# Fifteen gate and up weight units split at another address offset, in a hybrid decoder layer on one Trainium2 core

## The chip, the cores and the metric

The kernel runs on one core of a Trainium2 chip. The metric is the device time of one execution in microseconds, taken as the median of the runs. One execution was also recorded by the hardware profiler; its time stands beside its span (from the first to the last instruction).

## The reference, cut to what matters

One layer on 512 tokens of width 2048, in float32: a mixer (an RG-LRU and an RWKV-7 half), a feed-forward network of width 6144, a gated embedding, and norms. The change touches the first half of the feed-forward network:

```python
u = rmsnorm(h, ln_ffn[i])
gate = causal_dwconv(u @ w_gate[i], conv_f_w[i], conv_f_b[i])
h = h + (jax.nn.gelu(gate) * (u @ w_up[i])) @ w_down[i]
```

`w_gate` and `w_up` are 2048 by 6144 each.

## The kernel before, in words

**Precision.** Each product is made of three matmuls in a fast float32 format. An operand is split in a high part (ScalarE copies it to that format, line 138) and a low part (VectorE subtracts the high part from it, line 139). High times high, high times low and low times high are added up in PSUM.

**Stages.** Up to about 908 us the mixer runs, with 512-column matmuls of which the streamed operand is an activation tile `x` and the loaded weights are `whi` and `wlo` (`dense`, lines 173 to 177; in the gates of the RG-LRU, lines 1031 to 1035, the streamed tiles are `lxh` and `lxl`). From about 908 to 1870 us come gate and up. Then come the down projection (`product`, lines 1418 to 1420) and the gated embedding (`gate`, lines 1564 to 1566), to the end at 2575 us.

**Gate and up.** The products with `w_gate` and `w_up` are arranged so that seven products with sums and differences of operand blocks stand for eight plain ones. `gate_order` (line 1122) lists the work in 336 *units* (n, name): n is one of 48 blocks of 128 features, the name one of q5, p1, p4, p6, p7, p2, p3. In `part` (line 1288) a unit is 24 matmuls: for each of eight slices of 128 rows, the weights `whi` are loaded and stream past `xh`, loaded again and stream past `xl`, then `wlo` and `xh`. The streamed tiles `X` (named s in the profile) have 256 columns, and every matmul loads 128 by 128 weights first. The units run in this order on TensorE without a break.

**The feed of the weights.** `wqueue`, `wfill` and `wnext` (lines 105 to 151) hold a list of all weight units of the kernel in the order of their use. For a unit, a raw weight tile of 512 KB is loaded by a transfer of the SP queue, or made by `gate_unit` (line 1129): an addition on VectorE, or a transfer of GpSimd's queue that adds to what is in the tile. Then line 138 writes `whi` and line 139 `wlo`. In this stage three units are kept ahead (LOOK), in three buffers each for `whi` and `wlo` (HL). Every fourth unit (k % 4 == 3, counted from 0) has two tiles of its own, x12 and x15, in place of a buffer.

**The addresses.** A buffer of `whi` or `wlo` has 1088 columns of 4 bytes in each partition, and a unit needs 1024. `wview` (line 142) puts the unit at column `a` of the buffer, with `a` from a table `at` by the unit's place in the list. `ffn_items` (line 1191) fills that table, and line 1204 sets it for the gate and up units. In the compiled program all `whi` and `wlo` buffers start at 128 modulo 256 bytes, x12 and x15 too, and the streamed `X` tiles at 64. So with a = 0 the streamed data lies 64 bytes below the weights, modulo 256 (the *difference* minus 64); with a = 48 (192 bytes) the weights are at 64 as well, difference zero; with a = 56 (224 bytes) the weights are at 96, 32 above the streamed data. x12 and x15 always have minus 64.

In the mixer both `x` and the weights are at 128, difference zero, and `lxh` and `lxl` are at 160, 32 above the weights. In the down projection and the gated embedding the split weights are streamed and the activations are loaded. There a = 48 gives difference zero. In the last part a = 32 puts the streamed weights at 0, with the loaded tiles at 64, so minus 64; and two weight units with tiles of their own (s8, s11) are at 64, difference zero.

**What sets the order around the change.** The order of units is that of `gate_order`. The queue of weights follows it, and each split waits for the buffer of the unit three before it. Line 1204 changes nothing in order, number or size of instructions.

Of the kernel before, what the change touches and what calls it, by code (L numbers as in the profile page):

```python
# [90 lines left out]
class Builder:  # L91
# [1099 lines left out]
    def ffn_items(self):  # L1191
        A = self.A
        u = (128, 8, 128)
        r = []
        direct = {"p1": (0, 0), "p2": (0, 1), "p4": (1, 1)}
        self.gw = {}
        for k, (n, o) in enumerate(self.gate_order()):
            own = (("x12", "x15") if k % 4 == 3 else ())
            if o == "p2" or n == 0 and o in direct or n == 1 and o == "p1":
                i, j = direct[o]  # L1200
                r.append((A["wgu"][n // 2 * 2 + i, n % 2, j], u) + own)
            else:
                r.append((lambda n=n, o=o: self.gate_unit(n, o), u) + own)
        r = [(i, 48 if k in (12, 16, 20) or k % 56 == 4 else 0) for k, i in enumerate(r)]
        u = (128, 2, 512)
        self.d0, self.d1, self.dq, self.pn = {}, {}, {}, 0
        for lo, hi in GROUPS:
            for b in range(2):
                for i in ORDER:
                    for ch in range(lo, hi):  # L1210
                        if i == 5:
                            r.append(((A["wd"][ch, b, 1, 0], u), 48))
                        else:
                            r.append(((lambda ch=ch, c=ch - lo, b=b, i=i: self.down_unit(ch, c, b, i), u), 48))
        r += [((A["wd"][NCH - 1, cb % 2, kh, cb // 2], u), 48) for cb in (0, 2, 1, 3) for kh in range(2)]
        for cb in range(4):
            r += [((A["wpp"][cb], u), 0)]
            if cb < 3:
                r += [((A["wpg"][cb, i], u), 48) for i in KORDER[cb > 0]]
        r += [((A["wpg3"][0, i], (128, 4, 256)), 32) for i in range(2)]  # L1220
        r += [((A["wpg3"][1, 0, :, 2 * i:2 * i + 2], (128, 2, 256), ("s8", "s11")[i]), 0) for i in range(2)]
        r += [((A["wpg3"][0, i], (128, 4, 256)), 32) for i in range(2, 4)]
        r += [((A["wpg3"][1, i], (128, 4, 256)), 32) for i in range(1, 4)]
        return r
# [535 lines left out]
```

## Time and profile before

| | before |
|---|---|
| median of 3 runs | 2575.83 us |
| lowest and highest | 2571.14, 2579.5 us |
| the profiled execution | 2576.38 us |
| its span | 2574.6 us |
| its mean granted TensorE clock | 0.990 |
| ScalarE | 49% busy |
| GpSimd | 9% busy |
| HBM traffic over the span | 152 GB/s |

In a group of the profile, the tile names have lost their numbers: `mm<-s,whi` is a matmul that writes a PSUM tile mm, streams s and has whi loaded. A name x in the place of whi or wlo is x12 or x15, and wk is a second kind of PSUM tile. "128*128" is the size of the loaded weights, and behind it stand the streamed partitions and columns. A row of busy time by stretches has the length, then the busy time and the number of instructions of each engine, the granted clock, the share of the DMA engines and their rate. An instruction that begins before a stretch and ends in it is counted. A row of a timeline has the start, the duration and the instruction.

### The profile page before, as it was taken

To read this page: it belongs to the slowest core of one execution; us is meant where nothing else is said; L and a number is where in the kernel's file an instruction comes from. 1 tells how busy PE (TensorE), PEld (TensorE's weight loads), DVE (VectorE), ACT (ScalarE), POOL (GpSimd) and SP (SyncE) were. 2 spreads that over 40 slices of the span, in tenths; PEclk is the share of its full clock that TensorE was granted. 3 is DMA by queue.
4 is the path that set the end of the run, shared out by engine and by line. 5 is a ranking of instruction groups with operands and counts; after the bars stand their busy time and mean duration, and the time that the engine had idled before them with its cause. 6 is when DMAs were issued, how large, how long until landed. Compare 5 with 4: busy or idle time off the path is not lost.

```text
span 2574.6 us, 51613 instructions
## 1 busy us (share of the span) xinstructions
PE 2517.4 (98%) x21922; PEld 2220.6 (86%) x21922; DVE 1902.3 (74%) x2603; ACT 1248.8 (49%) x1735; POOL 228.0 (9%) x251
## 2 busy tenths in 40 slices
PE   9989999999999989999999999999999999999997
PEld 8767777777777889999999999999988877888887
DVE  5765775776585988888888888888876877896447
ACT  6563654557432644444444444444465453535345
POOL 0010100101031000000000000000000000000001
PEclk9999999999999999999999999999999999999998
DMA  7221222222342567767777677676778686843233
GB/s 256 91 74 59 87 79 68 79 81 73 92 145 83 163 202 196 190 170 192 197 183 190 167 196 194 182 191 181 206 223 240 184 239 177 248 121 122 92 94 111
DMA packets 131448, 393.76 MB, mean 153 GB/s; under 512 B 14481, under 2 KB 26769, under 8 KB 131217
## 3 DMA queue, kind: packets, MB, share of 16 engines
q1 hardware_dynamic: 96624, 299.22, 34.5%
q0 software_dynamic: 19872, 72.36, 16.8%
q10 hardware_dynamic: 14720, 18.88, 2.2%
q8 instruction: 171, 2.80, 0.4%
q14 instruction: 61, 0.49, 0.1%
HBM read 353.97 MB, written 36.44 MB: 152 GB/s over the span
## 4 chain that ended last, share of the span: by engine, by line
PE 59%; DVE 6%; DMA 3%; ACT 2%; issue 2%; POOL 0%; ACTq 0%; POOLq 0%; DVEq 0%; SPq 0%
PE mm L1293 8%; PE mm L1294 8%; PE mm L1292 8%; PE mm L1419 5%; PE mm L1420 5%; PE mm L1418 5%; PE wk L1293 3%; PE wk L1292 3%; PE wk L1294 3%; PE mm L1564 2%; PE mm L1565 2%; PE mm L1566 2%; DVE wlo L139 2%; DMA wraw<-wd 1%; PE mm L173 1%
## 5 line engine op out<-in xcount | busy, mean ns | idle before, releaser
L138 ACT ACTIVATE whi<-x 128x1024 fp32r<-128x1024 f32 x329 | 348.4, 1060 | 472.8 <-PE mm L1293 223.2
L139 DVE TENSOR_TENSOR wlo<-x,whi 128x1024 fp32r<-128x1024 f32 x329 | 401.8, 1222 | 134.2 <-ACT whi L138 130.7
L138 ACT ACTIVATE whi<-wraw 128x1024 fp32r<-128x1024 f32 (+1 forms) x229 | 233.2, 1018 | 388.8 <-PE mm L175 181.1
L1292 PE MATMUL mm<-s,whi 128*128 128x256 f32 x1432 | 403.4, 282 | 3.6 <-ACT whi L138 2.5
L139 DVE TENSOR_TENSOR wlo<-wraw,whi 128x1024 fp32r<-128x1024 f32 (+1 forms) x229 | 279.2, 1219 | 172.4 <-ACT whi L138 170.8
L1294 PE MATMUL mm<-s,wlo 128*128 128x256 f32 x1432 | 403.3, 282 | 0.8 <-DVE wlo L139 0.8
L1293 PE MATMUL mm<-s,whi 128*128 128x256 f32 x1432 | 403.2, 282 | 0.2 <-DVE s L157 0.2
L173 PE MATMUL mm<-x,whi 128*128 128x512 f32 x832 | 332.9, 400 | 2.3 <-DVE tmp L519 1.0
L177 PE MATMUL mm<-x,wlo 128*128 128x512 f32 x832 | 332.7, 400 | 0.0
L175 PE MATMUL mm<-x,whi 128*128 128x512 f32 x832 | 331.0, 398 | 0.0
L1292 PEld LDWEIGHTS mm<-s,whi 128*128 128x128 f32 x1432 | 275.5, 192 | 4.0 <-ACT whi L138 2.7
L1294 PEld LDWEIGHTS mm<-s,wlo 128*128 128x128 f32 x1432 | 269.7, 188 | 1.0 <-DVE wlo L139 1.0
L1419 PE MATMUL mm<-wlo,s 128*128 128x512 f32 x680 | 267.0, 393 | 3.4 <-DVE wlo L139 3.4
L1293 PEld LDWEIGHTS mm<-s,whi 128*128 128x128 f32 x1432 | 269.7, 188 | 0.4 <-DVE s L157 0.4
L1418 PE MATMUL mm<-whi,s 128*128 128x512 f32 x680 | 265.5, 392 | 3.0 <-ACT whi L138 3.0
L1420 PE MATMUL mm<-whi,s 128*128 128x512 f32 x680 | 266.3, 392 | 0.2
L173 PEld LDWEIGHTS mm<-x,whi 128*128 128x128 f32 x832 | 157.5, 189 | 38.1 <-issue 3.0
L177 PEld LDWEIGHTS mm<-x,wlo 128*128 128x128 f32 x832 | 157.2, 189 | 34.2 <-issue 1.9
L175 PEld LDWEIGHTS mm<-x,whi 128*128 128x128 f32 x832 | 157.4, 189 | 33.8 <-issue 1.8
L1158 POOL DMA_DIRECT2D x<-wgu x94 | 82.9, 882 | 936.6 <-DVE wlo L139 632.2
L1292 PE MATMUL wk<-s,whi 128*128 128x256 f32 x584 | 164.2, 281 | 1.3 <-DVE e L1318 1.3
L1293 PE MATMUL wk<-s,whi 128*128 128x256 f32 x584 | 164.1, 281 | 0.0
(579 smaller groups left out, 5417.7 us busy)
## 6 DMA issues: line engine op xcount, KB each, us to landing
x<-wgu SPq DMA_DIRECT2D x144, 512.0 KB, 4.2
x<-wgu POOLq DMA_DIRECT2D x94, 512.0 KB, 5.5
wraw<-wz SPq DMA_DIRECT2D x80, 512.0 KB, 3.5
wraw<-wgu SPq DMA_DIRECT2D x51, 512.0 KB, 4.2
x<-wd SPq DMA_DIRECT2D x49, 512.0 KB, 6.0
x<-wd POOLq DMA_DIRECT2D x44, 512.0 KB, 6.1
wraw<-wpg SPq DMA_DIRECT2D x31, 512.0 KB, 3.5
wraw<-wd SPq DMA_DIRECT2D x30, 512.0 KB, 4.5
```

The lines of the kernel that those rows point to most:

```text
L138: nc.scalar.activation(hi, raw, AF.Copy)
L139: nc.vector.tensor_tensor(lo, raw, hi.bitcast(F32), ALU.subtract)
L173: nc.tensor.matmul(ps, hi[:, k, :], xh, start=first and i == 0, stop=False)
L175: nc.tensor.matmul(ps, hi[:, k, :], xl, start=False, stop=False)
L177: nc.tensor.matmul(ps, lo[:, k, :], xh, start=False, stop=last and i == n - 1)
L1158: nc.gpsimd.dma_start(g["s"], src(0, 0 if u == "p6" else 1), accum_op=ALU.add)
L1292: TE.matmul(ps, wh[:, k, :], xh, start=k == 0, stop=False)
L1293: TE.matmul(ps, wh[:, k, :], xl, start=False, stop=False)
L1294: TE.matmul(ps, wl[:, k, :], xh, start=False, stop=k == 7)
L1418: TE.matmul(ps, x[0][:, k, ts_], w[0][:, k, :], start=first and k == 0, stop=False)
L1419: TE.matmul(ps, x[0][:, k, ts_], w[1][:, k, :], start=False, stop=False)
L1420: TE.matmul(ps, x[1][:, k, ts_], w[0][:, k, :], start=False, stop=last and k == 1)
```

## The change

Line 1204 is replaced:

```diff
-        r = [(i, 48 if k in (12, 16, 20) or k % 56 == 4 else 0) for k, i in enumerate(r)]
+        r = [(i, 56 if k // 4 in (3, 5, 7, 29, 57) and k % 4 < 3 else 0) for k, i in enumerate(r)]
```

Before, nine units have a = 48: 4, 12, 16, 20, 60, 116, 172, 228 and 284. After, none has. Fifteen have a = 56: 12 to 14, 20 to 22, 28 to 30, 116 to 118 and 228 to 230. Each of these five groups is followed by a unit with tiles of its own. All other gate and up units have a = 0.

## The prediction

> **What bounds the kernel now.** I read the page first, then busy time by stretches, then groups of instructions in the stretch that the change touches.
>
> ```profile
> span 2574.6 us, 51613 instructions
> PE 2517.4 (98%) x21922; PEld 2220.6 (86%) x21922; DVE 1902.3 (74%) x2603; ACT 1248.8 (49%) x1735; POOL 228.0 (9%) x251
> ```
>
> ```profile
> core 0: us, PE busy (x) PEld busy (x) DVE busy (x) ACT busy (x) POOL busy (x), PEclk, DMA share, GB/s
> 1000.00:1200.00 200.00, 200.00 (x1700) 200.00 (x1699) 164.61 (x182) 90.08 (x96) 17.57 (x20) 1.00 0.72 190
> 1200.00:1400.00 200.00, 200.00 (x1701) 200.00 (x1700) 163.60 (x181) 90.33 (x96) 18.46 (x21) 1.00 0.70 183
> ```
>
> The changed units run from about 908 to 1870 us. In there TensorE is busy 200 us of 200 at the full granted clock, VectorE 82%, ScalarE 45%, the DMA engines 0.7. The groups of the stretch 960 to 1866 us say who feeds whom:
>
> ```profile
> L1293 PE MATMUL mm<-s,whi 128*128 128x256 f32 x1364 | 383.3, 281 | 0.0
> L1294 PE MATMUL mm<-s,wlo 128*128 128x256 f32 x1364 | 383.3, 281 | 0.0
> ```
>
> ```profile
> L138 ACT ACTIVATE whi<-x 128x1024 fp32r<-128x1024 f32 x207 | 219.4, 1060 | 312.9 <-PE mm L1293 223.2 <-PE wk L1293 89.7
> ```
>
> ```profile
> L139 DVE TENSOR_TENSOR wlo<-x,whi 128x1024 fp32r<-128x1024 f32 x206 | 251.9, 1223 | 81.5 <-ACT whi L138 78.1
> ```
>
> The matmuls wait for nothing (0.0 before them). The split waits for TensorE to free a buffer (312.9 us before ScalarE's part), so the feed has room. The stage is as long as 336 units of 24 matmuls are at their own spacing, and nothing else ends last. A matmul's recorded 281 ns overlaps its neighbours; what counts is start to start. I get that by counting matmuls in stretches whose ends lie between two starts. Two in each count began before the stretch, so the spacing is the length over (count minus 2).
>
> ```profile
> core 0: us, PE busy (x), PEclk, DMA share, GB/s
> 1100.00:1240.00 140.00, 140.00 (x1191) 1.00 0.70 180
> 1248.54:1251.42 2.88, 2.88 (x26) 1.00 1.06 358
> 1251.42:1254.25 2.83, 2.83 (x26) 1.00 0.89 172
> 942.80:945.15 2.35, 2.35 (x22) 1.00 0.00 0
> 951.65:954.24 2.59, 2.59 (x24) 1.00 0.72 174
> 924.52:931.43 6.91, 6.91 (x63) 1.00 0.95 226
> 2513.73:2518.45 4.72, 4.72 (x42) 1.00 0.50 134
> 2521.06:2535.46 14.40, 14.40 (x129) 1.00 0.23 74
> 2538.15:2541.44 3.29, 3.29 (x31) 1.00 0.00 0
> 441.95:443.76 1.81, 1.81 (x10) 1.00 0.15 57
> 444.24:446.34 2.10, 2.10 (x11) 1.00 0.00 0
> ```
>
> All of them ran at clock 1.00. For the 256-column matmul the rows show three spacings that hold steady:
> - 140 us over 1189, 117.7 ns: the gate and up stage at difference minus 64, with none of the nine units in it. Rows 942.80 (117.5) and 951.65 (117.7), and 2513.73 at the end of the kernel (118.0), are the same.
> - 2.88 over 24, 120.0 ns: unit 116, one of the nine at difference zero. The next unit, row 1251.42, is back at 117.9.
> - 6.91 over 61, 113.3 ns, in the same stage, also at minus 64; and 14.40 over 127 and 3.29 over 29, 113.4 ns, in the last part of the kernel at minus 64.
>
> So minus 64 has two gaits, one 4% shorter than the other. Whichever TensorE falls into, it keeps until something disturbs it. From 951 to 1867 us nothing does but the units at zero, and it stays in the long one.
>
> **The change part by part.**
>
> What it removes: nine units at zero go to minus 64 (four of them, units 12, 20, 116 and 228, go to 32). At unchanged gait that is 2.88 − 2.83 = 0.05 us each, 0.45 us for nine. Nothing hides it, because TensorE sets the stage.
>
> What it adds: 15 units at difference 32. No 256-column matmul of before has that difference. The nearest rows are the two last of the list, with 512 columns: at difference zero 1.81 over 8, 226 ns; right behind, with the moving operand 32 above the weights, 2.10 over 9, 233 ns. That is about 7 ns more and no short gait in the stretch. Put on 113.3 this gives 120.3, the spacing of the units at zero, and I take 120: 24 × (120.0 − 117.7) = 0.055 us a unit, 0.8 us for 15. Bounds: below, the short gait holds inside the groups, 24 × 15 × (113.3 − 117.7) = −1.6 us; above, twice the 7 ns, 24 × 15 × (127 − 117.7) = +3.4 us. No instruction, wait or transfer is added or moved; the split of line 138 and 139 runs with another offset in the same buffer. If it cost ScalarE or VectorE more at another address, their idle time above covers it.
>
> So inside the units the whole change is worth under 4 us either way. What decides is the gait in which TensorE leaves a group. Two ways out of difference zero are in the trace. In the gate stage, row 1251.42: long gait (and the same behind the other units at zero from unit 12 on, eight of eight). In the last part each of four runs of 12 matmuls at zero is followed by matmuls at minus 64; the first:
>
> ```profile
> start us, us, engine line op out<-in xcount [idle before <-releaser]
> 2537.26 0.28 PE L1565 MATMUL mm<-s,s 128*128 128x256 f32 x1
> 2537.38 0.28 PE L1566 MATMUL mm<-s,s 128*128 128x256 f32 x1
> 2537.50 0.29 PE L1564 MATMUL mm<-whi,s 128*128 128x256 f32 x1
> 2537.62 0.28 PE L1565 MATMUL mm<-wlo,s 128*128 128x256 f32 x1
> 2537.74 0.28 PE L1566 MATMUL mm<-whi,s 128*128 128x256 f32 x1
> 2537.86 0.28 PE L1564 MATMUL mm<-whi,s 128*128 128x256 f32 x1
> 2537.97 0.28 PE L1565 MATMUL mm<-wlo,s 128*128 128x256 f32 x1
> 2538.09 0.28 PE L1566 MATMUL mm<-whi,s 128*128 128x256 f32 x1
> ```
>
> Steps of 120 ns become 110 to 120 within five matmuls, and row 2538.15 shows the short gait from there on. Same two differences, other result. What differs is which operand moved: here the streamed one went from 64 to 0, in the gate stage the weights go from 64 to 128. A start is therefore decided by where the streamed data and the weights stand at that moment, and a group that ends with the weights at 96 leaves from another place than one that ends at 64. After a wait it is open too:
>
> ```profile
> start us, us, engine line op out<-in xcount [idle before <-releaser]
> 923.77 0.38 PE L1294 MATMUL mm<-s,x 128*128 128x256 f32 x1 [0.63 <-DVE x L139]
> ...
> 951.40 0.36 PE L1292 MATMUL wk<-s,x 128*128 128x256 f32 x1 [0.72 <-DVE e L1318]
> ```
>
> After the first came 113.3, after the second 117.7. Counting by kind: long after 942.8, 951.4, 2513.4 and the units at zero in the gate stage; short after 923.8 and after the runs at zero in the last part. It is near a coin toss for one way out, and I put it a little above half for the short gait, since there are three groups close together and 72 matmuls give each of them time to settle.
>
> The sum for the short gait: units 15 to 335 are 321, less the 12 in the four later groups, 309 units × 24 × (117.7 − 113.3 = 4.4 ns) = 32.6 us less; the groups and the removed nine +0.8 − 0.45 = +0.4. Together −32.2 us.
>
> Can the feed follow? A unit then has 2.72 us instead of 2.83. VectorE's 164.61 us in 200 become 171, ScalarE's 90 become 94, the DMA share 0.72 becomes 0.75. The tightest is the weight that is added up in memory by a transfer of GpSimd's queue:
>
> ```profile
> x<-wgu POOLq DMA_DIRECT2D x90, 512.0 KB, 5.5
> ```
>
> It must land between two splits that are four units apart, 10.9 us then; 5.5 us in the median and the split's 1.06 + 1.22 leave 3 us. I cost that at nothing.
>
> The profiled execution took 2576.38 us, 1.8 us over its span, and lies 0.6 us over the median of the three runs (2575.83, from 2571.14 to 2579.5). From the profiled one the sum is 2544.2; from the median it is 2543.6, and I give 2544. The runs spread over 0.3%, so 7.7 us is what can be told from no change.
>
> On the rule that speaks against the change: the rows just used have spacing depend on the address of the weights, 120.0 against 117.9. The Trainium skill (TensorE: Matmul & The Clock Gate, Part 2, step 1) holds that TensorE has two independent read ports, so that loading the next weights takes nothing from the running matmul. By that rule both spacings would be equal and the change would do nothing; the trace disagrees by 2 ns a matmul.
>
> **The rivals.**
> - *The gait stays long.* Every exit is like row 1251.42: 15 units at 120 instead of nine, 2575.8 + 0.4 = 2576. For it: eight of eight in this stage. Against it: the exits at 2537.5 and the start at 923.8.
> - *Short for a part.* Only the group at unit 116 or 228 turns it, or a later one turns it back: 218 units × 0.106 = 23 us or 105 × 0.106 = 11 us less, 2553 or 2565.
> - *Slower: a third gait.* Behind a group TensorE at minus 64 keeps the 120 ns that it shows at zero: 309 × 24 × 2.3 ns = 17 us more, 2593. It decides from 7.7 us over 321 × 24 matmuls, 1.0 ns, so from 118.7 on. For it: at 444 us the 512-column matmuls kept 233 as long as the difference held. Against it: every settled stretch at minus 64 shows one of the two gaits.
> - *Addresses do nothing.* The 0.05 us at unit 116 would be chance, and the time 2575.8; eight equal units speak against it.
>
> **How the numbers follow.** Short gait from an early group 0.46, short for a part 0.11, long gait 0.34, addresses nothing 0.02, third gait 0.07. Faster by over 0.3%: 0.46 + 0.11 = 0.57. Within: 0.36. Slower: 0.07. The likeliest case alone: 2544 with −1.6 and +3.4 for the groups and ±4 for the runs, 2538 to 2551. The range over the cases reaches up to the long gait with the same additions, 2581, and leaves out the third gait.
>
> **What would show it.** In the changed profile a stretch of 140 us in this stage without a group should hold 140000/113.3 = 1235 matmuls and not 1189; the stage should end near 1834 us instead of 1867; units 116 to 118 should take about 2.88 us each. If the stretches before and after each group hold 1189, the groups don't turn the gait, and I am wrong by 32 us. If short stretches end at a wait on VectorE or a transfer, the feed was the step that failed.

## The result and the profile after

| | before | after |
|---|---|---|
| median of 6 runs each, one chip | 2574.16 us | 2541.42 us |
| lowest and highest | 2571.14, 2579.5 us | 2533.88, 2574.53 us |
| the profiled execution | 2576.38 us | 2544.37 us |

The ratio of the times is 0.9862, with a 95% interval from 0.984 to 0.9884: 1.4% faster. The runs of the changed kernel fall into two groups some 32 us apart, and since a ratio leaves out runs that lie over 1.5% above the fastest, the text also gives the number of runs in each group. Here five lie at 2533.9 to 2544.6 us and one, 2574.53, where the kernel before lies.

The head of the page after:

```profile
span 2542.6 us, 51613 instructions
PE 2486.8 (98%) x21922; PEld 2188.8 (86%) x21922; DVE 1898.9 (75%) x2603; ACT 1250.1 (49%) x1735; POOL 228.2 (9%) x251
```

The same instructions, and TensorE busy for 30.6 us less. Where these went is read from stretches cut at the same places of the program. First the kernel before: its gate and up stage to the start of unit 12 and from there to its end, then, with TensorE alone, the down projection and the last part. In the first two rows stand the length, busy time and number of instructions of TensorE, weight loads, VectorE, ScalarE and GpSimd, then clock, DMA share and GB/s.

```profile
908.53:954.20 45.67, 38.52 (x305) 37.17 (x304) 34.67 (x48) 18.24 (x28) 4.87 (x5) 0.96 0.73 210
954.20:1870.56 916.36, 916.36 (x7779) 916.36 (x7778) 754.60 (x837) 416.82 (x445) 79.98 (x91) 1.00 0.71 187
...
1870.56:2364.53 493.97, 487.37 (x2186) 1.00 0.71 198
2364.53:2574.60 210.07, 193.29 (x1043) 0.97 0.30 98
```

The same stretches of the kernel after:

```profile
908.88:953.04 44.16, 38.51 (x305) 37.33 (x304) 34.60 (x47) 17.95 (x27) 4.85 (x5) 0.96 0.75 220
953.04:1836.15 883.11, 883.11 (x7779) 883.11 (x7777) 750.49 (x837) 417.58 (x445) 79.82 (x91) 1.00 0.74 194
...
1836.15:2332.35 496.20, 488.75 (x2185) 1.00 0.71 198
2332.35:2542.60 210.25, 193.31 (x1043) 0.97 0.31 98
```

From unit 12 on the stage takes 883.11 us in place of 916.36, 33.25 less, with the same 7779 matmuls and TensorE busy throughout. The rest comes to +1.2: −1.5 ahead of unit 12, +2.2 in the down projection, +0.5 elsewhere.

Inside that stretch, TensorE alone (length, busy time and count, clock, DMA share, GB/s; two of each count began before the stretch):

```profile
951.16:953.04 1.88, 1.88 (x18) 1.00 0.89 131
953.04:961.56 8.52, 8.52 (x74) 1.00 0.49 133
961.56:964.30 2.74, 2.74 (x26) 1.00 0.34 88
964.30:975.18 10.88, 10.88 (x98) 1.00 0.90 238
...
1100.00:1240.00 140.00, 140.00 (x1237) 1.00 0.74 196
...
1237.02:1245.54 8.52, 8.52 (x74) 1.00 0.91 259
1245.54:1256.41 10.87, 10.87 (x98) 1.00 0.69 178
```

Unit 11 ends in the long gait (1.88 over 16, 117.5 ns). The first group, units 12 to 14, takes 118.3 ns a matmul (8.52 over 72). Unit 15 needs five or so steps to change over, and units 16 to 19 run at 113.3 (10.88 over 96). The 140 us that held 1189 matmuls before hold 1235. The group at unit 116 costs 118.3 as well, and behind it TensorE is back at 113.3.

How the feed stands, in the groups from 960 to 1834 us:

```profile
L1293 PE MATMUL mm<-s,whi 128*128 128x256 f32 x1365 | 377.2, 276 | 0.0
...
L139 DVE TENSOR_TENSOR wlo<-x,whi 128x1024 fp32r<-128x1024 f32 x206 | 251.4, 1220 | 71.5 <-ACT whi L138 68.3
L138 ACT ACTIVATE whi<-x 128x1024 fp32r<-128x1024 f32 x206 | 218.9, 1063 | 285.1 <-PE mm L1293 199.7 <-PE wk L1293 74.7 <-DMA x<-wgu 8.5
```

The matmuls still wait for nothing, and the split still waits for TensorE, 285 us where it was 313.

### The profile page after: what moved, and what is told of

Read it like the earlier page. It is cut to its first block, busy times and chain, and to the rows that moved or that the text cites. A ratio compares the mean times of both kernels' runs of the same rounds, so it can differ in the third digit from the quotient of the medians.

```text
span 2542.6 us, 51613 instructions
## 1 busy us (share of the span) xinstructions
PE 2486.8 (98%) x21922; PEld 2188.8 (86%) x21922; DVE 1898.9 (75%) x2603; ACT 1250.1 (49%) x1735; POOL 228.2 (9%) x251
## 4 chain that ended last, share of the span: by engine, by line
PE 58%; issue 5%; DVE 4%; DMA 3%; ACT 1%; POOL 0%; ACTq 0%; POOLq 0%; DVEq 0%; SPq 0%
PE mm L1294 8%; PE mm L1293 8%; PE mm L1292 8%; PE mm L1420 5%; PE mm L1419 5%; PE mm L1418 5%; PE wk L1292 3%; PE wk L1294 3%; PE wk L1293 3%; PE mm L1564 2%; PE mm L1565 2%; PE mm L1566 2%; DMA wraw<-wd 2%; DVE wlo L139 1%; ACT whi L138 1%
## 5 line engine op out<-in xcount | busy, mean ns | idle before, releaser
L139 DVE TENSOR_TENSOR wlo<-x,whi 128x1024 fp32r<-128x1024 f32 x329 | 401.1, 1220 | 121.0 <-ACT whi L138 117.5
L1292 PE MATMUL mm<-s,whi 128*128 128x256 f32 x1432 | 396.1, 277 | 1.0 <-ACT s L156 0.9
L1294 PE MATMUL mm<-s,wlo 128*128 128x256 f32 x1432 | 396.0, 277 | 0.8 <-DVE wlo L139 0.8
L1293 PE MATMUL mm<-s,whi 128*128 128x256 f32 x1432 | 396.0, 277 | 0.2 <-DVE s L157 0.2
L1292 PEld LDWEIGHTS mm<-s,whi 128*128 128x128 f32 x1432 | 268.9, 188 | 1.5 <-ACT s L156 1.1
L1294 PEld LDWEIGHTS mm<-s,wlo 128*128 128x128 f32 x1432 | 268.9, 188 | 1.0 <-DVE wlo L139 1.0
L1293 PEld LDWEIGHTS mm<-s,whi 128*128 128x128 f32 x1432 | 269.0, 188 | 0.4 <-DVE s L157 0.4
L1292 PE MATMUL wk<-s,whi 128*128 128x256 f32 x584 | 162.3, 278 | 2.9 <-DVE e L1318 2.9
L1294 PE MATMUL wk<-s,wlo 128*128 128x256 f32 x584 | 162.1, 278 | 0.0
```

The lines of the kernel that those rows point to most:

```text
L139: nc.vector.tensor_tensor(lo, raw, hi.bitcast(F32), ALU.subtract)
L1292: TE.matmul(ps, wh[:, k, :], xh, start=k == 0, stop=False)
L1293: TE.matmul(ps, wh[:, k, :], xl, start=False, stop=False)
L1294: TE.matmul(ps, wl[:, k, :], xh, start=False, stop=k == 7)
```

## The experiments

Every kernel differs from the changed one in line 1204 alone (one of them needs two lines there), so the instructions and their order are the same in all. A *quad* is four units, number k // 4; a *group* is the three units of a quad that have a buffer, between two units with tiles of their own; those always stand at minus 64. The prediction and the expectations call the change's difference 32; by the sign of the table below it is minus 32 (a = 56). Only where an expectation has the streamed data 64 above the weights does 32 mean a = 32.

One reading is needed first. The long gait isn't one thing. In it every third weight load is recorded a little longer, and which line has it differs. Busy time and mean of the loads, for unit 11 after its start in the changed kernel:

```profile
L1294 PEld LDWEIGHTS wk<-s,x 128*128 128x128 f32 x6 | 1.1, 188 | 0.0
L1293 PEld LDWEIGHTS wk<-s,x 128*128 128x128 f32 x5 | 1.0, 192 | 0.0
L1292 PEld LDWEIGHTS wk<-s,x 128*128 128x128 f32 x5 | 0.9, 188 | 0.0
```

and for the stretch from 960 to 1866 us in the kernel before:

```profile
L1292 PEld LDWEIGHTS mm<-s,whi 128*128 128x128 f32 x1364 | 261.9, 192 | 0.0
L1293 PEld LDWEIGHTS mm<-s,whi 128*128 128x128 f32 x1364 | 256.1, 188 | 0.0
L1294 PEld LDWEIGHTS mm<-s,wlo 128*128 128x128 f32 x1363 | 255.9, 188 | 0.0
```

I call these long 1293 and long 1292, by the line with 192 ns. Their spacing is the same 117.8 ns; in the short gait all loads show 188.

**No group at all.**

```diff
-        r = [(i, 56 if k // 4 in (3, 5, 7, 29, 57) and k % 4 < 3 else 0) for k, i in enumerate(r)]
+        r = [(i, 0) for k, i in enumerate(r)]
```

> The removal alone: every gate and up unit at minus 64, no unit at zero and none at 32. Theory (the groups at 32 turn TensorE to the short gait): nothing turns it, the stretch from unit 12 to the down projection keeps the 117.8 ns of the gait that it fell into after the last wait, about 336 x 24 x 117.8 ns less the nine units' 0.05 us each, so 2575 us, and a stretch of 140 us holds 1189 matmuls. Rival (the nine units at zero held TensorE in the long gait): 113.3 ns without any group, 1235 matmuls in 140 us, 2541 us. Between them: the wait at about 950 us decides by chance, and the runs differ by 33 us.

Median 2573.98 us of 10 runs, 2 of them short (2532.5 and 2538.4) and 8 at 2568.7 to 2577.2; before, on the same chip, 2571.01. The profiled run was a long one:

```profile
1100.00:1240.00 140.00, 140.00 (x1191) 1.00 0.70 179
```

So taking the units away from difference zero isn't enough. In the profile TensorE keeps the long gait in which it starts unit 11. The two short runs, which have no profile, have the time of a kernel that starts and stays in the short one.

**The same five groups at difference zero.**

```diff
+        r = [(i, 48 if k // 4 in (3, 5, 7, 29, 57) and k % 4 < 3 else 0) for k, i in enumerate(r)]
```

> The same fifteen units at difference zero in place of 32. Theory (where the weights stand when a group ends decides): zero leaves to the long gait however many units the group has, 120.0 ns in the groups, 117.8 behind each, 15 x 0.05 = 0.8 us over a kernel without groups, 2576 us. Rival (72 matmuls of any other difference are enough, 32 is nothing special): 113.3 ns behind the first group, 2542 us.

Median 2571.13 us, ratio 1.0 (0.999 to 1.0011), and all 10 runs long (2567.4 to 2573.9). The end of unit 11, the first group, and units 16 to 19:

```profile
946.70:948.52 1.82, 1.82 (x18) 1.00 0.76 135
948.52:957.15 8.63, 8.63 (x74) 1.00 0.61 155
959.98:971.29 11.31, 11.31 (x98) 1.00 0.80 222
```

This is the clearest row of the study. TensorE came into the group in the short gait (1.82 over 16, 113.8 ns), ran at 119.9 in it, and left in the long one (11.31 over 96, 117.8). Units at zero don't let the gait fall as it may: they set the long one. With five groups or with the nine units of before, no run is short. A single unit can change the kind, too: in the kernel before, unit 11 runs in long 1294,

```profile
L1294 PEld LDWEIGHTS wk<-s,x 128*128 128x128 f32 x8 | 1.5, 192 | 0.0
```

and behind unit 12, the only one at zero between, it is long 1292. A single unit at zero met in the short gait is in no profile. All this is seen in the gate and up stage. In the last part, where the weights are streamed, short matmuls follow the runs at zero (row 2538.15 of the prediction, 113.4 ns), and no run tested why.

**Only the last group, units 228 to 230.**

```diff
+        r = [(i, 56 if k // 4 == 57 and k % 4 < 3 else 0) for k, i in enumerate(r)]
```

> Only the fifth group, units 228 to 230, is at 32; all else at minus 64. Theory: 117.8 ns up to unit 228 and 113.3 from unit 231 on, 105 units x 0.106 us = 11 us less than without a group, about 2564 us. Rival (the gait comes from the start of the stage, the groups only keep it): no change at unit 231, one spacing on both sides.

2571.29 us in one run. The four units ahead of the group, the group, and four units behind:

```profile
1550.78:1562.09 11.31, 11.31 (x98) 1.00 0.82 246
1562.09:1570.61 8.52, 8.52 (x74) 1.00 0.82 221
1570.61:1581.92 11.31, 11.31 (x98) 1.00 0.67 189
```

Long ahead (117.8), 118.3 in the group, long behind. A group that ends with the weights at 96 does not by that leave into the short gait. My theory had said that it does, and it fell here. What differs from the changed kernel's first group is the long gait on the way in; here it was long 1294:

```profile
L1294 PEld LDWEIGHTS mm<-s,wlo 128*128 128x128 f32 x904 | 173.6, 192 | 0.0
```

**All offsets in one launch.** Sixteen groups, each at one of the seven offsets other than minus 64 (number of the quad: a).

```diff
+        g = {3: 56, 10: 8, 14: 16, 18: 24, 22: 32, 26: 40, 30: 48, 34: 56, 42: 40, 46: 32, 50: 24, 54: 16, 58: 8, 62: 56, 66: 48, 70: 56}
+        r = [(i, g.get(k // 4, 0) if k % 4 < 3 else 0) for k, i in enumerate(r)]
```

> The first group as in the change, then groups of three units at seven offsets of 8 to 56 columns, twice, with units at minus 64 between them. Theory: each difference has a spacing of its own in the group, and each turns TensorE to one gait behind it whichever gait it had before: 32 (offset 56) to 113.3, zero (offset 48) to 117.8; the other five are open. Rival (a group only shakes TensorE loose, and the gait behind it is chance): the two passes of one offset leave different gaits behind. Time between 2541 and 2576 us.

2559.05 us in one run. The group with a = 32, and the one with a = 48 with the four units behind its quad:

```profile
1162.42:1170.58 8.16, 8.16 (x74) 1.00 0.87 261
...
1249.70:1258.33 8.63, 8.63 (x74) 1.00 0.72 189
1261.16:1272.47 11.31, 11.31 (x98) 1.00 0.61 143
```

At a = 32 the group runs at the short gait itself (8.16 over 72, 113.3 ns). At zero it is 119.9 and then long, again out of the short gait. All other groups leave short when they come in short. The theory fell at a = 56: twice it came in short and left short, twice it came in long behind a group at zero and left long. So an offset alone doesn't set the gait behind it.

**The changed kernel again**, to count its runs.

> The changed kernel once more, for how often it falls into the short gait. What the kernels so far showed: the long gait repeats every three matmuls, with one step that is longer than the other two, and that step sits behind the first, second or third matmul of a triple. A group at 32 led from the second to the short gait (the changed kernel), from the first to the third and from the third to the third (the kernels with the late group and with all offsets), and from the short gait to the short gait. Theory (the group maps each state to one state, and the five groups are no five tries): a run is short when it is short or of the second kind at unit 12, so some half of the runs are near 2541 us and the others near 2574, with one spacing from unit 31 to the end in any profile. Rival (each group is a try of its own): nearly all runs are near 2541 us, and some between, where a later group turned it.

Median 2540.95 us, ratio 0.9895 (0.9858 to 0.9933). Four of six runs short (2536.9 to 2543.6), two not (2566.29, 2578.74). With the first six that is 9 of 12. In its profiled run unit 11 was already in the short gait, and the group kept it. 9 of 12 lies between the half of the theory and the nearly all of the rival; but no run lies between the two times, and in neither profile does a later group turn the gait.

**Which way out, from which way in.** Zero groups set the long gait again and again, and groups at other offsets follow each.

```diff
+        r = [(i, {3: 48, 5: 8, 8: 48, 10: 16, 13: 48, 15: 24, 18: 48, 20: 32, 23: 48, 25: 40, 28: 48, 30: 56, 32: 8, 35: 48, 37: 56, 39: 16, 42: 48, 44: 56, 46: 24, 49: 48, 51: 56, 53: 32, 56: 48, 58: 56, 60: 40, 63: 48, 65: 56, 67: 56, 69: 56, 72: 40, 75: 56, 78: 32}.get(k // 4, 0) if k % 4 < 3 else 0) for k, i in enumerate(r)]
```

> Groups of three units at zero put TensorE in the long gait of the first kind; behind each comes a group at one of the other six offsets, and then the same with a group at 32 between them, which should leave the third kind. Theory: the state behind a group is a function of the offset and of the state before it, so 32 from the first kind gives the third each time, 32 three times in a row from there stays long, and offset 40 from the third kind gives 113.3 again as it did in the kernel with all offsets. Rival (chance at each exit): equal pairs of state and offset give different gaits. For offsets 8, 16, 24 and 32 from the long gait nothing is known; at 32 (the streamed data 64 above the weights) either 113.3 within the group and behind it, or 117.8. Time between 2541 and 2576 us, near 2570 as most stretches are long by design.

2561.4 us in one run. Pairs of rows from it: a = 16 out of a long gait and what follows; a = 56 and what follows; a = 8 right behind and what follows; a later a = 56 and what follows.

```profile
1030.15:1038.70 8.55, 8.55 (x74) 1.00 0.66 157
1041.43:1052.31 10.88, 10.88 (x98) 1.00 0.87 230
...
1253.25:1261.77 8.52, 8.52 (x74) 1.00 0.67 162
1264.59:1275.90 11.31, 11.31 (x98) 1.00 0.60 145
1275.90:1284.35 8.45, 8.45 (x74) 1.00 0.86 255
1287.08:1297.96 10.88, 10.88 (x98) 1.00 0.67 160
...
1667.94:1676.46 8.52, 8.52 (x74) 1.00 0.89 249
1679.29:1690.60 11.31, 11.31 (x98) 1.00 0.66 166
```

Every group at a = 56 that comes in long leaves long, whichever of the two kinds it met, also three in a row; the one that came in short (units 300 to 302) left short. Behind the groups at the other five offsets apart from zero stands 10.88 over 96, the short gait, or 10.87. So the theory held. The time is under the 2570 us expected, since all five of these offsets turned the gait. The loads show what a = 56 did at 1253 us: ahead of it L1292 has the long load, behind it L1294.

```profile
L1292 PEld LDWEIGHTS mm<-s,whi 128*128 128x128 f32 x17 | 3.3, 192 | 0.0
```

```profile
L1294 PEld LDWEIGHTS mm<-s,wlo 128*128 128x128 f32 x24 | 4.6, 192 | 0.0
```

The two launches together, from the recorded starts of their 48 groups: the spacing in the group and the gait behind it, by the gait that it came in with. Where no number of times stands, it is one to three, and all agree.

| a | streamed data minus weights, mod 256 | in the group, ns | came in short | came in long 1292 | came in long 1294 |
|---|---|---|---|---|---|
| 8 | −96 | 120.0, from long 117.3 to 117.4 | short | short | short |
| 16 | −128 | 118.5 to 118.7 | short | short | short |
| 24 | 96 | 119.9 | short | short | short |
| 32 | 64 | 113.3, from long 117.7 | short | short | short |
| 40 | 32 | 116.6 to 116.8 | short | short | short |
| 48 | 0 | 119.9 to 120.0 | long 1292, 12 times | long 1292, once | – |
| 56 | −32 | 118.3 | short, 3 times | long 1294, 8 times | long 1294, twice |

So the change's offset is the only one apart from zero that doesn't turn these two long gaits. Long 1293, the one in which the profiled execution of the changed kernel came to its first group, did not occur in either launch. In this stage the streamed data stood at 64 throughout, so the rows don't tell the difference from the weights' own address. For two of them the last part does, where the loaded tiles are at 64 both times: the prediction's rows have 120 ns there at difference zero and 113.4 at minus 64.

**The first group alone, twice, and once more none.** The second time, this kernel and the one without any group ran on one chip.

```diff
+        r = [(i, 56 if k // 4 == 3 and k % 4 < 3 else 0) for k, i in enumerate(r)]
```

> Only the first group, units 12 to 14, with a = 56 (weights 32 above the streamed data); the four later groups at minus 64. Theory (a group at this offset keeps the gait, save for the one long kind that the first group meets; groups 2 to 5 do nothing but cost 12 x 24 x 5 ns = 1.4 us): the same mixture as the changed kernel, most runs 2533 to 2543 and a third or fewer at 2564 to 2578, median 2539. Rival (each of the five groups is a fresh try): with one try in place of five clearly more long runs, half or more, and a median over 2560.

> The kernel with the first group alone once more, beside the one without any group. Theory (the first group turns one long kind that unit 11 may start in): over two thirds of the runs at 2532 to 2545, the others at 2564 to 2579. Rival (the group only keeps): the same share as without any group, at most half.

> The kernel of the first experiment once more, no gate and up unit off minus 64, beside the one with the first group alone on one chip. Theory (unit 11 starts in the short gait in about 5 profiles of 11, here nothing disturbs what it starts in; the first group adds the turn of one of the long kinds): a mixture with between a fifth and a half of the runs at 2532 to 2545 and the others at 2564 to 2579; fewer short ones than with the first group. Rival (the first group does nothing but keep, and only taking the units away from difference zero counts): the same share of short runs as the kernel with the first group.

The first group alone: 2542.16 us with 4 of 4 runs short, ratio 0.987 (0.9854 to 0.9885); then 2536.04, 4 of 4, ratio 0.9861 (0.9844 to 0.9877). No group, beside the second: 2569.91, 2 of 10 short (2531.1 and 2536.5). The second profile with the first group again shows the turn, and again out of long 1293; unit 11, the group, and units 16 to 19:

```profile
949.52:951.40 1.88, 1.88 (x18) 1.00 0.85 109
951.40:959.92 8.52, 8.52 (x74) 1.00 0.53 143
962.66:973.54 10.88, 10.88 (x98) 1.00 0.88 236
```

```profile
L1293 PEld LDWEIGHTS wk<-s,x 128*128 128x128 f32 x5 | 1.0, 192 | 0.0
```

Over all runs: before, 0 of 58 runs short (lowest 2564.8); no group, 4 of 20; the first group, alone or with the others, 17 of 20. The rival in which five groups are five tries falls: with one group there are no fewer short runs than with five. So does the one in which the group only keeps.

**An offset that turned both long gaits of the table.** One group at a = 40:

```diff
+        r = [(i, 40 if k // 4 == 3 and k % 4 < 3 else 0) for k, i in enumerate(r)]
```

> One group only, units 12 to 14, with a = 40 (streamed data 32 above the weights); all other gate and up units at minus 64. Theory (the way out of a group is set by its offset and by the gait on entry; 40 leaves into the short gait from both long ones that the one-launch map showed, 32 above turned neither of these): every run in the short gait from unit 15 on, none in the long one; median 2538 us, all runs 2532 to 2546, ratio 0.987; profile with units 15 to 335 at 113.3 ns. Rival (the gait is a matter of chance in each run, whatever the group): about a third of the runs or more at 2564 to 2579 as in the changed kernel.

2541.01 us, ratio 0.9862 (0.9842 to 0.9882), 4 of 4 runs short (2532.9 to 2542.3). Its profiled run came to the group in long 1292, which a = 56 didn't turn in the map, and left short:

```profile
943.76:945.64 1.88, 1.88 (x18) 1.00 0.91 122
945.64:954.05 8.41, 8.41 (x74) 1.00 0.63 153
956.78:967.66 10.88, 10.88 (x98) 1.00 0.90 235
```

```profile
L1292 PEld LDWEIGHTS wk<-s,x 128*128 128x128 f32 x5 | 1.0, 192 | 0.0
```

And a = 32 wherever a unit has a buffer:

```diff
+        r = [(i, 32 if k % 4 < 3 else 0) for k, i in enumerate(r)]
```

> All gate and up units without tiles of their own at a = 32 (streamed data 64 above the weights), every fourth unit at minus 64. Theory (from the short gait 32 runs at 113.3 ns, from the long one at 117.8, and every way out of it to a unit at minus 64 ends in the short gait): 113.3 ns from unit 15 at the latest and in all runs; median 2537 us, all runs 2531 to 2545, ratio 0.987. Rival (252 changes of offset are 252 chances to fall into the long gait, or the changes themselves cost): over 117 ns for a good part of the units, 2560 us or more.

2539.35 us, ratio 0.9868 (0.9849 to 0.9886), 4 of 4 short (2535.6 to 2543.6). From unit 12 on the stage takes 881.3 us, the shortest of all:

```profile
1100.00:1240.00 140.00, 140.00 (x1238) 1.00 0.75 195
```

Some 160 changes of offset behind unit 12 cost nothing. Both versions are as fast as the change's short runs, and of their 8 runs none is long, where the change has 3 of 12. The medians are too close to call a winner; and by the number of long runs they can't be told from the first group alone either, which had none in 8. What they have more is that the table shows no way for them to leave long; out of long 1293 no profile has either of them.

## Why the prediction was right, and where it wasn't

The forecast was 2544 us; the profiled execution took 2544.37 and the median of the runs was 2541.42. Point by point:

- **TensorE's spacing is the length of the stage.** Right. From unit 12 on TensorE is busy all the time in both kernels, and the stage's difference is the spacing's.
- **Two gaits at minus 64, 117.7 and 113.3.** Right in size. That the long one comes in kinds which answer differently to a group was not seen, although the rows of the loads (192 against 188 ns) were there to be read in the profile of before.
- **Units at 32 take 120 ns.** Mis-sized: 118.3, whichever gait they came from. The rows at 441.95 and 444.24 that it went by have the streamed operand 32 above the weights, and the change has it 32 below; in the sweep the two differ, 116.7 and 118.3. So the units cost 15 × 24 × (118.3 − 117.8) = +0.2 us over the long gait in place of +0.8.
- **The sum, −32.2.** Measured from unit 12 on: −33.25. Its terms are 309 units × 24 × 4.5 ns (11.31 − 10.88 = 0.43 us over 96 matmuls) = about −33, the groups +0.2, and the eight units at zero in that stretch −0.4. The whole execution is 32.0 shorter, since the rest gave 1.2 back, of which the 2.2 of the down projection are from one execution each and weren't followed.
- **The feed follows.** Right. The waits of TensorE from 953 to 1836 us are empty in the changed kernel.
- **The way out of a group.** This is the step that decided, and its reason failed. The prediction said that a start "is decided by where the streamed data and the weights stand at that moment", so that a group ending with the weights at 96 leaves from another place, and that three groups close together give "each of them time to settle". The late group ended at the same place and stayed long; groups 2 to 5 do nothing but cost, 881.7 us from unit 12 to the stage's end with the first alone against 883.1 with five. What the gait behind a group goes by is the offset together with the gait on the way in. At a = 56 the short gait stays, long 1293 turned both times it was seen, long 1292 and 1294 never did. So the close hit is in part luck: the profiled execution came to its first group in the one long kind that was seen to turn, and in 6 of 13 profiles unit 11 ran in one of the other two.
- **What the removal is worth.** Also missed. The nine units were counted at 0.45 us, and "eight of eight" long exits from difference zero were taken as a sample of a coin. In this stage they are a rule: all 18 groups at zero left long 1292, 13 of them out of the short gait. So the gain has two parts that need each other. The units at zero must go, or every group's work is undone at the next of them; and something must bring in the short gait, which the first group does for one kind on the way in.
- **The long gait as rival, 0.34.** Neither always nor never. The same program takes the long gait's time in 3 of 12 runs.
- **Short for a part.** Not seen: both profiles of the changed kernel keep 113.3 at minus 64 from unit 16 to the end of the stage, and no run's time lies between.
- **Addresses do nothing.** Wrong: the sweep has four spacings and more with nothing else changed.
- **Slower by a third gait.** No stretch at minus 64 shows a third spacing.

On the Trainium skill's two independent read ports (TensorE: Matmul & The Clock Gate, Part 2, step 1), by which the loading of weights takes nothing from the running matmul: the sweep has the same instructions at the same clock with 113.3, 116.7, 118.3 and 119.9 ns, by the weights' offset alone. Read as the prediction reads it, the rule gives one spacing for all, and the trace differs from that by up to 6.6 ns a matmul. That it is the loads that cost this time is not shown.

**What stays open.** Thirteen profiles show unit 11 starting short five times, in long 1292 four times, and in long 1293 and 1294 twice each. By the table 7 of 13 would then be short behind a first group at a = 56, and 17 of 20 runs were. Whether the unprofiled runs start otherwise, or a long 1292 or 1294 turns at unit 12 as they didn't later, no run here tells: both turns out of long 1293 were at unit 12, and no profile has a = 56 there out of another long kind, so the kind and the place aren't separated. What in TensorE or its memory makes the gaits isn't shown either; the table is what was seen, not a mechanism.

## What to carry to other kernels

Where matmuls run back to back, count start to start over a stretch without waits, and compare stretches that should be equal: two steady values for the same instruction mean a state that persists, and then the thing to find is what sets it. Look for the few instructions that set it as well as for those that you hope will clear it; nine units of 336, priced at half a microsecond, kept every run from a gain of 33 us. And run such a kernel several times before you believe one profile: prefer the version that reaches the good state from every way in that you have seen.

## What the runs showed of the hardware that was not expected

- The start-to-start time of the 256-column matmul with a weight load each, at the full granted clock, changed with where the weights lie against the streamed data, modulo 256 bytes: with the streamed data at 64, 113.3 ns at streamed minus weights 64 (out of the short gait), 116.7 at 32, 118.3 at −32, 120.0 at 0, and 113.3 or 117.8 at −64.
- At −64 it has a memory: in the kernel without a group the long gait held from unit 12 to the end of the stage, 916 us and 7776 matmuls.
- In the long gait exactly one of the three loads of a cycle is recorded at 192 ns and the others at 188. Which one it is goes with whether 72 matmuls at −32 turn it: two of two out of long 1293, none of eight out of long 1292, none of three out of long 1294.
